# A two-layer decoder trunk: h and two of four column blocks of x turned by DMA transposes, operand tiles on multiples of 512 bytes, order from a two-way walk

## The chip, the cores and the metric

The kernel runs on one core of one Trainium2 chip. The metric is the device time of one execution in microseconds, lower is better. Five engines matter: TensorE (PE; its weight loads are listed apart as PEld), VectorE (DVE), ScalarE (ACT), GpSimd (POOL, hardly used here) and SyncE (SP), which only issues DMAs. Data come from HBM into the on-chip memory SBUF; products land in eight PSUM banks.

## What is computed

256 tokens of 2048 columns go through two layers. Layer 0 mixes tokens by causal pooling means, layer 1 by differential attention; each is followed by a SwiGLU feed-forward with 5632 inner columns. All sub-layers take a normalised input and add to x; a last norm ends it.

```python
for i in range(DEPTH):                              # 2 layers
    hn = rmsnorm(h, norm_mix[i])
    mix = pool_mixer(hn, ...) if i % 2 == 0 else diff_attention(hn, w_qkv, ..., w_o)
    h = h + mix
    h = h + swiglu(rmsnorm(h, norm_ffn[i]), w_gate[i], w_up[i], w_down[i])
return rmsnorm(h, final_norm)

def swiglu(h, wg, wu, wd):
    return (jax.nn.silu(h @ wg) * (h @ wu)) @ wd
```

Everything is float32, so the kernel splits each operand into a high and a low part in the fp32r format and multiplies high by high, high by low and low by high.

## The kernel before

**A group of products.** All large products go through `group` (L335). A group has 8 steps (6 in the short down-projection); each step takes one pair of 128-row blocks of the contraction, loads one MiB of weights into `raw` (L307, SP's queue, three buffers), splits it into `whi` (ScalarE, L313) and `wlo` (VectorE, L314), and multiplies. A plain step has 8 block products, 24 matmuls of 128 x 512. A step "by seven" uses a scheme of Strassen's kind: 7 block products, 21 matmuls, but VectorE makes sums of the weights first (`tsum`, L319 to L321) and their low parts (`tlo`, L328), ScalarE their high parts (`thi`, L327). `GATE_UP`, `SEVEN`, `SEVEN_DOWN` and the like say which steps of a group go by seven. `combined` (L395) adds the seven sums up from the PSUM banks into four tiles c (L401 to L411).

**The operand side.** The stationary operand is the activations, turned so that the contraction lies on the partitions. For x it is `xp`/`xq`, one tile for each pair of blocks, made by `transposed` (L470) from `x_tok`; for the hidden layer it is `h`, made from the tiles c after silu and product (L677, L678). Both use `pair` (L445): four TensorE transposes of 128 x 128 into a PSUM bank (L450), then either the high and the low part directly (L454, L455, or with a gain L442, L443) or, for a step by seven, an evacuation to a tile e with eight slots (L463), three VectorE sums in it (L464 to L466), a cast and a subtraction (L467, L468).

**The stages.** The pooling layer comes first. A feed-forward (L657) runs in three chunks of 4, 4 and 3 gate-and-up groups; after each chunk come the two halves (o = 0 and 1) of the down-projection over that chunk's h, 8 steps each, 6 in the last chunk. After the last chunk x is updated, one column block of 512 at a time (j = 2o + b), its squares are summed (`square_sum`, L428), and the block is turned for the next stage. Attention has four groups for q and k, two for v, and two halves of the output projection, after which x is updated and turned in the same way (L827 to L834).

**The order.** TensorE, VectorE, ScalarE and SP work in order. `in_order_of_need` (L226) fixes that order before the kernel is built: `steps_of` (L104) reads the dependences out of the program, `walk` (L162) plays it forward with assumed durations and a rank, and `due` (L213) gives each instruction a limit from TensorE's order. Two rounds are tried, TensorE and SP keep the program's rank, and the best order becomes fixed dependences. `Step` (L68) holds the assumed durations: `lasts` until the result is there, `holds` until the engine takes its next instruction.

**Tiles.** `dist_sb` and `ones` are constants of the whole kernel, `small`, `counts` and `sq` are small tiles or scratch; where they lie shifts the addresses of the operand tiles behind them.

Of the kernel before, what the change touches and what calls it, by code (L numbers as in the profile page):

```python
# [10 lines left out]
F32 = mybir.dt.float32  # L11
F32R = mybir.dt.float32r
AF = mybir.ActivationFunctionType
# [16 lines left out]
ROUNDS = 2  # L30
# [24 lines left out]
A22, A21, A11, A12, S1, S3, S2, S4 = range(8)  # L55
T1, T3, T2, T4 = range(4)

# [7 lines left out]
PER_MIB = 2500  # L65


class Step:  # L68

    def __init__(self, k, ins=None):  # L70
        self.k, self.ins, self.engine = k, ins, ins.engine if ins else POOL
        self.dma = bool(ins) and ins.opcode == "DMACopy"
# [6 lines left out]
        if self.dma:  # L79
            bytes_ = 4 * math.prod(c for _, c in ins.outs[0].ap)  # L80
            self.share = PER_MIB * bytes_ / 2 ** 20
            self.holds, self.lasts = (60 if self.engine == ACT else 330), LANDING + self.share
        elif self.engine == PE:
            n = size(ins.outs[0])
            one = 110 if ins.is_transpose else 14 + n / 2.4 if "float32r" in str(ins.ins[0].dtype) else 14 + n / 0.6
            self.holds, self.lasts = one, one + 163
        elif self.engine == DVE:
            if ins.opcode == "TensorScalarPtr":
                self.lasts = 185 + n / 0.96 if n > 8 else 159
            else:  # L90
                self.lasts = 152 + n / (1.92 if ins.opcode == "TensorCopy" else 0.96)
            self.holds = max(self.lasts - 80, 60)
        elif self.engine == ACT:
            self.lasts = 165 + n * 0.852
            if ins.opcode == "Activation" and any(hasattr(a, "ap") for a in list(ins.ins)[1:]):
                self.lasts += 100
            self.holds = max(self.lasts - 30, 60)
            if len(ins.outs) > 1:
                self.lasts, self.holds = self.lasts + 190, self.lasts + 160
        else:  # L100
            self.holds = self.lasts = 400


def steps_of(instructions):  # L104
# [3 lines left out]
    for ins in instructions:  # L108
# [15 lines left out]
        for writes, args in ((False, ins.ins), (True, ins.outs)):  # L124
            for a in args:
# [4 lines left out]
                first = ap.offset % dims[0][0]  # L130
                last = first + sum((c - 1) * s for s, c in dims[1:])
                alone = writes
                if t.space == PSUM:
                    first, last, alone = 0, 511, True
# [78 lines left out]
def due(steps, start):  # L213

    by_start = sorted(steps, key=lambda s: start[s.k])
    at, clock = {}, 0.0
    for s in by_start:
        if s.engine == PE:
            at[s.k], clock = clock, clock + s.holds
    limit = [0.0] * len(steps)  # L220
    for s in reversed(by_start):
        limit[s.k] = min([limit[k] - s.lasts - SIGNAL[steps[k].engine] for k in s.after] + [at.get(s.k, clock)])
    return limit


def in_order_of_need(tc):  # L226
# [19 lines left out]
def trunk_kernel(ctx, tc, x_n, gains, scale_in, final_in, subln, lam_in, band, counts_in, dist,  # L246
# [31 lines left out]
    dist_sb = const.tile([P, 2 * P], F32, name="dist_sb")  # L278
    ident = const.tile([P, P], F32, name="ident")
    ones = const.tile([P, P], F32, name="ones")  # L280
    nc.vector.memset(ones, 1.0)
# [146 lines left out]
    def square_sum(ss, t, j):  # L428
# [16 lines left out]
    def pair(dst, src, gains, seven):  # L445

        ps = aux((P, 2, 2, P))
        for i in range(2):
            for t in range(2):
                nc.tensor.transpose(ps[:, i, 1 - t if seven else t], src(i, t), ident)  # L450
# [11 lines left out]
        for i, at in ((0, slice(A21, A11 + 1)), (1, slice(A22, A12 + 1, A12 - A22))):  # L462
            nc.scalar.activation(e[:, at], ps[:, i], AF.Copy, scale=1.0 if gains is None else gains[i])  # L463
        nc.vector.tensor_tensor(e[:, S1:S3 + 1], e[:, A21:A11 + 1], e[:, A22:A21 + 1], ALU.subtract)  # L464
# [3 lines left out]
        nc.vector.tensor_tensor(dst[:, 1], e, f32(dst[:, 0]), ALU.subtract)  # L468

# [9 lines left out]
    with tc.tile_pool(name="start", bufs=1, reuse_waits="tile") as st:  # L479

        warm = tmp.tile([P, 8], F32, name="warm", bufs=1)
# [9 lines left out]
        counts = st.tile([P, 8], F32, name="counts")  # L491
# [26 lines left out]
        def squares(j):  # L518
            for t in range(2):
                square_sum(ss_in, t, j)  # L520
# [57 lines left out]
        def residual(g):  # L578

            cols = slice(g * 512, (g + 1) * 512)  # L580
            for t in range(2):
# [3 lines left out]
                square_sum(ss, t, g)  # L585
# [43 lines left out]
    nc.sync.dma_start(out=dist_sb, in_=dist)  # L629

    def finish(cs, ys, final_sb, ss):

        for t in range(2):
            part = tmp.tile([P, 64], F32, name="part", bufs=2)
            nc.vector.tensor_reduce(part[:, 0:1], ss[:, t, 0:2], AX.X, ALU.add)
            for b in range(2):
                for h in range(2):
# [3 lines left out]
                    sq = tmp.tile([P, 512], F32, name="sq", bufs=1)  # L641
                    at = 1 + 2 * b + h
                    nc.scalar.activation(sq[:, :S], x_at(t, first, S), AF.Square, accum_out=part[:, at:at + 1])
# [13 lines left out]
    def ffn(layer, xq, ss, next_op, next_gain):  # L657
# [3 lines left out]
        with tc.tile_pool(name=f"ffn{layer}", bufs=1, reuse_waits="tile") as hp:  # L661
            g0 = 0
            ys = []
            for c, n in enumerate(CHUNKS):
# [6 lines left out]
                for g in range(g0, g0 + n):  # L671
# [3 lines left out]
                    for t in range(2):  # L675
                        gate, up = cs[t]
                        nc.scalar.activation(gate, gate, AF.Silu, scale=r[:, t:t + 1])  # L677
                        nc.vector.scalar_tensor_tensor(up, up, r[:, t:t + 1], gate, ALU.mult, ALU.mult)  # L678
                    for i in range(2):
                        at = 2 * (g - g0) + i  # L680
                        ht = hp.tile(pair_shape(at in SEVEN_DOWN), F32R, name="h", tag=f"h{at}")
                        pair(ht, lambda k, t: cs[t][1][:, (2 * i + k) * P:(2 * i + k + 1) * P], None, at in SEVEN_DOWN)
                        hp_tiles.append(ht)
                for o in range(2):
# [13 lines left out]
                    for b, t in ((0, 0), (0, 1), (1, 0), (1, 1)):  # L698
                        j = 2 * o + b
                        nc.vector.tensor_tensor(x_at(t, j * 512), cs[t][b], x_at(t, j * 512), ALU.add)  # L700
                        if last:
                            square_sum(ss_next, t, j)
# [6 lines left out]
                        if last and t and next_op is not None:  # L709
                            transposed(next_op, j, next_gain, SEVEN_QKV)  # L710
# [8 lines left out]
    with tc.tile_pool(name="attn", bufs=1, reuse_waits="tile") as ap_, ExitStack() as heads:  # L719
        hq = heads.enter_context(tc.tile_pool(name="qk_sums", bufs=1, reuse_waits="tile"))  # L720
        at = heads.enter_context(tc.tile_pool(name="attn_tmp", bufs=2, reuse_waits="tile"))
        small = ap_.tile([P, 64], F32, name="small")
# [84 lines left out]
        for g in range(2):  # L807
            order, by_seven = LATE if g else EARLY
            cs = scaled(combined(group([(xp[p], p in by_seven, w_v[g, p]) for p in order], op_, bufs=1), op_), (r_col, r_col))
            for h in range(4 * g, 4 * g + 4):  # L810
# [6 lines left out]
                for t in range(2):  # L817
                    sq = tmp.tile([P, 512], F32, name="sq", bufs=1)[:, :E]
# [8 lines left out]
        for g in range(2):  # L827
            cs = combined(group([(oT[p], p in SEVEN_O, w_o[g, p]) for p in range(NP)], op_, bufs=1), op_)
            for b in range(2):
                j = 2 * g + b  # L830
                for t in range(2):
                    nc.vector.tensor_tensor(x_at(t, j * 512), cs[t][b], x_at(t, j * 512), ALU.add)
                    square_sum(ss_next, t, j)
                transposed(xq, j, 4, SEVEN)  # L834
# [91 lines left out]
```

## Time and profile before

| what | value |
|---|---|
| time, median of 3 runs | 1822.0 us (1821.96 to 1822.05) |
| the profiled execution | 1821.8 us |
| its span, first to last instruction | 1819.9 us |
| granted TensorE clock | 0.998 |
| TensorE busy | 1806.3 us, 8153 matmuls and transposes |
| VectorE busy | 1686.3 us |
| ScalarE busy | 1084.0 us |
| read from HBM | 352.9 MB |

The page of the profile gives busy times and their share of the span, the chain of work that ended last, and the costliest groups of instructions. A row of a group reads: line, engine, operation, what it writes and reads, shapes and count; then busy time and the mean duration of one in ns; then the idle time of the engine before them and what ended it. The durations of matmuls overlap, so the mean duration of one is more than the turn it takes in TensorE's stream. Windows give each engine's busy time in stretches of the span. A row of waits gives total, times and longest.

### The profile page before, as it was taken

The page shows a single profiled execution, that of the slowest core. Times are in us where ns is not written, and L with a number is a line of the kernel's source. Part 1 is how long each engine was busy: PE and PEld are TensorE (multiplying, and loading weights), DVE is VectorE, ACT ScalarE, POOL GpSimd, SP SyncE. Part 2 cuts the span into 40 slices and gives each one's busy share as a digit, 9 for nine tenths or more (in the row PEclk, how much of TensorE's full clock was granted, in tenths as well). Part 3 has the DMA queues.
Part 4 walks back from the last instruction along what each step waited for, and adds up shares of the span by engine and source line. Part 5 has one row for each costly group of instructions (what it writes and reads, how often), then busy time and mean ns, then how long its engine had stood idle before and what let it go on. Part 6 is the DMA issues. An engine that isn't in the chain of part 4 may idle for free.

```text
span 1819.9 us, 21122 instructions
## 1 busy us (share of the span) xinstructions
PE 1806.3 (99%) x8153; PEld 1487.6 (82%) x8153; DVE 1686.3 (93%) x1875; ACT 1084.0 (60%) x1170; POOL 0.7 (0%) x6
## 2 busy tenths in 40 slices
PE   9999999999999999999999999999999999999997
PEld 7888888888888888888888888888888888888886
DVE  7999999999999999989997889999999999999996
ACT  7656654565645566666666766665655556445663
POOL 0000000000000000000000000000000000000000
PEclk9999999999999999999999999999999999999999
DMA  6555555455555455635544445555555455555562
GB/s 267 208 185 207 187 208 208 185 208 215 201 209 187 182 208 185 225 145 185 185 176 172 184 165 194 196 208 185 214 207 203 185 208 192 210 222 192 196 220 109
DMA packets 50932, 356.37 MB, mean 196 GB/s; under 512 B 6160, under 2 KB 6288, under 8 KB 8464
## 3 DMA queue, kind: packets, MB, share of 16 engines
q1 hardware_dynamic: 49968, 353.40, 52.7%
q10 hardware_dynamic: 864, 1.63, 0.2%
q8 instruction: 64, 1.05, 0.2%
q14 instruction: 36, 0.29, 0.1%
HBM read 352.90 MB, written 2.10 MB: 195 GB/s over the span
## 4 chain that ended last, share of the span: by engine, by line
PE 98%; DVE 1%; ACT 1%; issue 0%; DVEq 0%; ACTq 0%
PE b L380 92%; PE b L450 2%; PE b L559 1%; PE b L555 1%; PE b L767 1%; PE b L798 0%; DVE wlo L314 0%; PE b L813 0%; PE b L485 0%; PE b L814 0%; PE b L530 0%; PE b L815 0%; DVE c L402 0%; DVE c L403 0%; PE b L752 0%
## 5 line engine op out<-in xcount | busy, mean ns | idle before, releaser
L380 PE MATMUL b<-whi,xp 128*128 128x512 f32 x2654 | 850.3, 392 | 0.4 <-ACT xp L467 0.3
L313 ACT CAST whi<-raw 128x1536 fp32r<-128x1536 f32 (+1 forms) x328 | 573.0, 1747 | 349.3 <-PE b L380 270.4
L314 DVE TENSOR_TENSOR wlo<-raw,whi 128x1536 fp32r<-128x1536 f32 (+1 forms) x328 | 681.3, 2077 | 69.6 <-ACT whi L313 68.4
L380 PEld LDWEIGHTS b<-whi,xp 128*128 128x128 f32 x2654 | 496.4, 188 | 104.9 <-DVE c L408 2.7
L380 PE MATMUL b<-wlo,xp 128*128 128x512 f32 x1327 | 520.1, 392 | 0.1
L327 ACT CAST thi<-tsum 128x1024 fp32r<-128x1024 f32 x254 | 266.3, 1052 | 183.9 <-DVE tsum L321 96.1
L380 PE MATMUL b<-whi,h 128*128 128x512 f32 x1108 | 349.2, 390 | 0.0
L328 DVE TENSOR_TENSOR tlo<-tsum,thi 128x1024 fp32r<-128x1024 f32 x254 | 306.5, 1216 | 2.3 <-ACT thi L327 2.0
L380 PEld LDWEIGHTS b<-wlo,xp 128*128 128x128 f32 x1327 | 249.2, 188 | 50.9 <-DVE wlo L314 0.5
L380 PE MATMUL b<-thi,xp 128*128 128x512 f32 x744 | 248.4, 390 | 0.0
L380 PEld LDWEIGHTS b<-whi,h 128*128 128x128 f32 x1108 | 207.6, 188 | 42.6 <-DVE c L408 0.2
L380 PE MATMUL b<-wlo,h 128*128 128x512 f32 x554 | 216.0, 390 | 0.1
L380 PEld LDWEIGHTS b<-thi,xp 128*128 128x128 f32 x744 | 139.4, 188 | 28.8 <-ACT thi L327 0.2
L319 DVE TENSOR_TENSOR tsum<-raw 128x1024 f32<-128x1024 f32 x127 | 154.5, 1216 | 0.6
L380 PE MATMUL b<-tlo,xp 128*128 128x512 f32 x372 | 144.9, 389 | 0.0
L380 PEld LDWEIGHTS b<-wlo,h 128*128 128x128 f32 x554 | 104.0, 188 | 21.9 <-DVE wlo L314 0.5
L320 DVE TENSOR_TENSOR tsum<-tsum,raw 128x512 f32<-128x512 f32 x127 | 86.7, 683 | 0.6
L321 DVE TENSOR_TENSOR tsum<-tsum,raw 128x512 f32<-128x512 f32 x127 | 86.7, 682 | 0.5
L380 PEld LDWEIGHTS b<-tlo,xp 128*128 128x128 f32 x372 | 69.8, 188 | 15.1
L380 PE MATMUL b<-thi,h 128*128 128x512 f32 x240 | 78.7, 389 | 0.0
L677 ACT ACTIVATE c<-c,r_tok 128x512 f32<-128x512 f32 x44 | 31.9, 724 | 63.1 <-DVE c L403 36.1
L380 PE MATMUL b<-whi,oT 128*128 128x512 f32 x216 | 69.0, 395 | 0.0
(148 smaller groups left out, 1230.7 us busy)
## 6 DMA issues: line engine op xcount, KB each, us to landing
raw<-w_gu SPq DMA_DIRECT2D x176, 1024.0 KB, 4.8
raw<-w_down SPq DMA_DIRECT2D x88, 1024.0 KB, 4.8
raw<-w_qk SPq DMA_DIRECT2D x32, 1024.0 KB, 4.8
raw<-w_v SPq DMA_DIRECT2D x16, 1024.0 KB, 4.8
raw<-w_o SPq DMA_DIRECT2D x16, 1024.0 KB, 4.7
x_tok<-x_n SPq DMA_DIRECT2D x4, 512.0 KB, 7.2
w<-pool_w SPq DMA_DIRECT2D x4, 512.0 KB, 7.7
raw<-pool_w SPq DMA_DIRECT2D x2, 1024.0 KB, 11.2
```

The lines of the kernel that those rows point to most:

```text
L313: nc.scalar.copy(hi[:, lo_block:], raw[:, lo_block:])
L314: nc.vector.tensor_tensor(lo[:, lo_block:], raw[:, lo_block:], f32(hi[:, lo_block:]), ALU.subtract)
L319: nc.vector.tensor_tensor(s, raw[:, B11:B22 + 1], raw[:, B12:B12 + 1].broadcast_to([P, 2, 512]), ALU.add)
L320: nc.vector.tensor_tensor(t[:, 0], s[:, 0], raw[:, B22], ALU.add)
L321: nc.vector.tensor_tensor(t[:, 1], t[:, 0], raw[:, B21], ALU.add)
L327: nc.scalar.copy(hi, t)
L328: nc.vector.tensor_tensor(lo, t, f32(hi), ALU.subtract)
L380: nc.tensor.matmul(ps[b], x, y[:, block], start=first, stop=(left[b] == 0))
L450: nc.tensor.transpose(ps[:, i, 1 - t if seven else t], src(i, t), ident)
L555: nc.tensor.matmul(yp[g][t], a[:, rows], w_pool[g][:, at], start=(at == 0), stop=(at == 3))
L559: nc.tensor.matmul(yp[g][t], u, v[:, at], start=(at == 0 and j == 0), stop=(at == 3 and j == 2))
L677: nc.scalar.activation(gate, gate, AF.Silu, scale=r[:, t:t + 1])
```

## The change

**Transposes by DMA.** A float32 number is moved as two 16-bit halves. `flip` copies 512 columns of a 128-token tile on ScalarE into another tile, all first halves ahead of all second halves, and SP issues a DMA that transposes the 1024 half words in blocks of 128 into a tile `turned`. `pair_of_words` puts the halves together again: ScalarE copies them from `turned` into e, with the two halves side by side, and from there the high and low parts are made as before. All of h goes this way, in both layers. Of x, the column blocks of the first half of the projection (j = 0 and 1) after the first feed-forward and after the attention go this way; j = 2 and 3 and the blocks after the pooling still use `pair`.

```diff
+    def flip(turned, t, gate, up):
+        halves_ = half_words(gate)
+        nc.scalar.copy(halves_.rearrange("p (w n) -> p w n", w=2), half_words(up).rearrange("p (n w) -> p w n", w=2))
+        nc.sync.dma_start_transpose(out=turned[:, t].rearrange("p w b n -> p (w b) n"), in_=halves_)
+
+    def pair_of_words(dst, turned, i, seven, gains=None):
+        e = tmp.tile([P, 8, P], F32, name="e", bufs=1)
+        words = half_words(e).rearrange("p b (n w) -> p b n w", w=2)
+        if seven:
+            for k, at in enumerate(PLACES):
+                nc.scalar.copy(words[:, at], turned[:, :, :, 2 * i + k].rearrange("p t w n -> p t n w"))
+                if gains is not None:
+                    nc.scalar.activation(e[:, at], e[:, at], AF.Copy, scale=gains[k])
+            seven_of(dst, e)
+            return
+        for k in range(2):
+            nc.scalar.copy(words[:, 2 * k:2 * k + 2], turned[:, :, :, 2 * i + k].rearrange("p t w n -> p t n w"))
+        both = e[:, :4].rearrange("p (k t) n -> p k (t n)", k=2)
+        if gains is not None:
+            for k in range(2):
+                split(dst[:, k], both[:, k], gains[k])
+            return
+        nc.scalar.copy(dst[:, :, 0], both)
+        nc.vector.tensor_tensor(dst[:, :, 1], both, f32(dst[:, :, 0]), ALU.subtract)
+
+    def turned_by_transfer(pool, xp, j, gain, seven, spare):
+        turned = pool.tile([P, 2, 2, 4, P], U16, name="turned")
+        for t in range(2):
+            flip(turned, t, spare[t], x_tok[:, j, t])
+        for i in range(2):
+            p = 2 * j + i
+            pair_of_words(xp[p], turned, i, p in seven, [gain_sb[:, gain, 2 * p + k:2 * p + k + 1] for k in range(2)])
...
                         nc.vector.scalar_tensor_tensor(up, up, r[:, t:t + 1], gate, ALU.mult, ALU.mult)
+                        if t == 0:
+                            turned = hp.tile([P, 2, 2, 4, P], U16, name="turned")
+                        flip(turned, t, gate, up)
                     for i in range(2):
...
-                        pair(ht, lambda k, t: cs[t][1][:, (2 * i + k) * P:(2 * i + k + 1) * P], None, at in SEVEN_DOWN)
+                        pair_of_words(ht, turned, i, at in SEVEN_DOWN)
...
-                            transposed(next_op, j, next_gain, SEVEN_QKV)
+                            if o:
+                                transposed(next_op, j, next_gain, SEVEN_QKV)
+                            else:
+                                turned_by_transfer(hp, next_op, j, next_gain, SEVEN_QKV, [cs[0][b], cs[1][b]])
...
-                transposed(xq, j, 4, SEVEN)
+                if g:
+                    transposed(xq, j, 4, SEVEN)
+                else:
+                    turned_by_transfer(op_, xq, j, 4, SEVEN, [cs[0][b], cs[1][b]])
```

The slots of e are renumbered so that the two token halves of a block stand in the order that the transfer writes:

```diff
-A22, A21, A11, A12, S1, S3, S2, S4 = range(8)
+A12, A11, A21, A22, S3, S1, S2, S4 = range(8)
```

**Places of tiles.** The scratch tile `sq` goes; the squares are written over tiles that are done with (in the last stage over the PSUM bank just read). `dist_sb` and `ones` move from the constants into the pools of the stages that use them (the DMA of dist with it), and `small` and `counts` become 128 columns wide, so that what follows them lies on a multiple of 512 bytes.

```diff
-    dist_sb = const.tile([P, 2 * P], F32, name="dist_sb")
...
-        sq = tmp.tile([P, 512], F32, name="sq", bufs=1)
         nc.scalar.activation(sq, x_at(t, j * 512), AF.Square, accum_out=ss[:, t, j:j + 1])
...
-        counts = st.tile([P, 8], F32, name="counts")
+        counts = st.tile([P, 128], F32, name="counts")[:, :8]
...
-                    nc.scalar.activation(sq[:, :S], x_at(t, first, S), AF.Square, accum_out=part[:, at:at + 1])
+                    nc.scalar.activation(cs[t][b][:, mine], x_at(t, first, S), AF.Square, accum_out=part[:, at:at + 1])
...
-        small = ap_.tile([P, 64], F32, name="small")
+        small = ap_.tile([P, 128], F32, name="small")
```

**The order.** `due` gives way to `latest`, which plays the program backward from its end with the same assumed durations, each engine taking one instruction at a time, and so gives each instruction the latest place that it can have. Up to eight rounds go backward and forward; in each, two ranks are tried, one that keeps TensorE and SP in the program's order and one that ranks them by need too. `Step` gets durations for the transposing DMA (SP is held 1290 ns; it lands 1000 ns and a share of 14 ns for each 2048 half words later) and 80 ns more for ScalarE copies with more than three dimensions.

```diff
-ROUNDS = 2
+ROUNDS = 8
...
+        if turns:
+            self.share = TURN_TILE * n * P / 2048
+            self.holds, self.lasts = 1290, 1000 + self.share
...
+    last = start
     for _ in range(ROUNDS):
-        limit = due(steps, start)
-        rank = [float(s.k) if s.engine in (PE, SP) else limit[s.k] for s in steps]
-        again, span = walk(steps, rank)
+        need = latest(steps, last)
+        both = [[float(s.k) if s.engine in (PE, SP) else need[s.k] for s in steps], need]
+        last, span = min((walk(steps, r) for r in both), key=lambda w: w[1])
         if span < end:
-            start, end = again, span
+            start, end = last, span
```

More of the change, by code (lines that the diff above doesn't have):

```diff
@@ L65 @@
 PER_MIB = 2500
+TURN_TILE = 14
 class Step:
@@ L129, in steps_of @@
                 t, dims = ap.tensor, [tuple(d) for d in ap.ap]
-                first = ap.offset % dims[0][0]
-                last = first + sum((c - 1) * s for s, c in dims[1:])
+                each = mybir.dt.size(a.dtype)
+                first = ap.offset % dims[0][0] * each
+                last = first + sum((c - 1) * s for s, c in dims[1:]) * each + each - 1
                 alone = writes
                 if t.space == PSUM:
-                    first, last, alone = 0, 511, True
+                    first, last, alone = 0, 2047, True
                 if t.name not in seen:
@@ L210, in walk, with latest @@
     return start, max(free.values())
[L213 to L223, printed above, removed]
+def latest(steps, start):
+    missing = [len(s.after) for s in steps]
+    ready, place = [0.0] * len(steps), [0.0] * len(steps)
+    engines = (PE, DVE, ACT, SP, POOL)
+    free = {e: 0.0 for e in engines}
+    able, coming = {e: [] for e in engines}, {e: [] for e in engines}
+    for s in steps:
+        if not s.after:
+            heapq.heappush(coming[s.engine], (0.0, s.k))
+    for _ in steps:
+        now, e = min((free[e] if able[e] else max(free[e], coming[e][0][0]), i)
+                     for i, e in enumerate(engines) if able[e] or coming[e])
+        e = engines[e]
+        while coming[e] and coming[e][0][0] <= now:
+            k = heapq.heappop(coming[e])[1]
+            heapq.heappush(able[e], (-start[k], -k))
+        s = steps[-heapq.heappop(able[e])[1]]
+        place[s.k] = free[e] = now + s.holds
+        for k in s.before:
+            b = steps[k]
+            if b.engine != e or b.dma:
+                after = b.lasts + SIGNAL[e] - (0 if b.dma else b.holds)
+            elif e == DVE or e == ACT and k in s.reads:
+                after = b.lasts + SETTLES[e] - b.holds
+            else:
+                after = 0.0
+            ready[k] = max(ready[k], place[s.k] + after)
+            missing[k] -= 1
+            if not missing[k]:
+                heapq.heappush(coming[b.engine], (ready[k], k))
+    end = max(place)
+    return [end - p for p in place]
 def in_order_of_need(tc):
@@ L449, in pair @@
             for t in range(2):
-                nc.tensor.transpose(ps[:, i, 1 - t if seven else t], src(i, t), ident)
+                nc.tensor.transpose(ps[:, i, t], src(i, t), ident)
         if not seven:
@@ L721, in trunk_kernel @@
         at = heads.enter_context(tc.tile_pool(name="attn_tmp", bufs=2, reuse_waits="tile"))
-        small = ap_.tile([P, 64], F32, name="small")
+        small = ap_.tile([P, 128], F32, name="small")
+        dist_sb = ap_.tile([P, 2 * P], F32, name="dist_sb")
+        nc.sync.dma_start(out=dist_sb, in_=dist)
+        ones = all_ones(ap_)
         qs_col, subln_sb, lam_sb, lp, le, neg_lam, gs = (
```

39 lines of the change are left out of this document (25 added, 14 removed).

## The prediction

> **What bounds the kernel now.** I read the page first: its busy times, its slices and its chain.
>
> ```profile
> span 1819.9 us, 21122 instructions
> PE 1806.3 (99%) x8153; PEld 1487.6 (82%) x8153; DVE 1686.3 (93%) x1875; ACT 1084.0 (60%) x1170; POOL 0.7 (0%) x6
> ...
> PEclk9999999999999999999999999999999999999999
> ...
> q1 hardware_dynamic: 49968, 353.40, 52.7%
> ...
> PE 98%; DVE 1%; ACT 1%; issue 0%; DVEq 0%; ACTq 0%
> ```
>
> TensorE is on 98% of the chain that ended last, at full granted clock, and it is idle for only 1819.9 - 1806.3 = 13.6 us. VectorE, at 93%, is close behind; ScalarE and the DMA rings have room. So what leaves TensorE's queue shortens the run, as long as VectorE can keep up with the shorter time. To see both I cut the span at the starts of the groups of products (a group is 6 or 8 loads of weights) and asked for busy time in these windows.
>
> ```profile
> core 0: us, PE busy (x) PEld busy (x) DVE busy (x) ACT busy (x) POOL busy (x), PEclk, DMA share, GB/s
> 85.70:127.40 41.70, 41.70 (x189) 34.57 (x188) 40.34 (x41) 25.01 (x22) 0.00 (x0) 1.00 0.54 197
> ...
> 211.80:254.20 42.40, 42.40 (x193) 35.09 (x192) 41.17 (x43) 23.59 (x21) 0.00 (x0) 1.00 0.54 199
> 254.20:295.70 41.50, 41.50 (x185) 34.38 (x184) 37.87 (x37) 20.90 (x16) 0.00 (x0) 1.00 0.55 203
> ...
> 421.10:463.50 42.40, 42.40 (x192) 35.11 (x191) 40.02 (x41) 24.48 (x22) 0.00 (x0) 1.00 0.54 198
> ...
> 588.30:630.00 41.70, 41.70 (x189) 34.40 (x188) 40.52 (x40) 24.91 (x22) 0.00 (x0) 1.00 0.56 202
> ...
> 672.60:704.90 32.30, 32.30 (x148) 26.73 (x147) 31.52 (x36) 19.20 (x20) 0.00 (x0) 1.00 0.55 196
> 704.90:738.00 33.10, 33.10 (x156) 27.52 (x155) 32.67 (x39) 23.48 (x31) 0.00 (x0) 1.00 0.52 191
> ...
> 1070.60:1114.50 43.90, 43.90 (x203) 36.47 (x202) 39.74 (x42) 25.93 (x33) 0.00 (x0) 1.00 0.60 222
> ...
> 1810.50:1819.90 9.40, 0.00 (x0) 0.00 (x0) 3.68 (x12) 1.95 (x6) 0.00 (x0) 0.64 0.55 212
> ```
>
> In each of these but the last, TensorE's busy time is the whole window. VectorE has 41.70 - 40.52 = 1.2 us left in a gate-and-up group with four sevens (588.30), and 0.4 us in 704.90. The last window is the tail without products; with it, 13.6 - 9.4 = 4.2 us of TensorE idle time remain in all the rest.
>
> **The change, part by part.** *TensorE's transposes.* The rows by form show them:
>
> ```profile
> L450 PE MATMUL b<-ident,c 128*128 128x128 f32 x176 | 26.3, 272 | 0.0
> ...
> L450 PE MATMUL b<-ident,x_tok 128*128 128x128 f32 x96 | 14.0, 273 | 0.0
> ```
>
> 176 is 22 groups x 2 pairs x 4 blocks: all of h. Of the 96 on x, 32 follow the pooling, 32 the first feed-forward and 32 the attention; the change takes two of four column blocks of the last two, 32 in all. Durations overlap, so I price them by windows. 211.80 and 254.20 are the two halves of the same down-projection, each 3 steps of 21 products and 5 of 24, 183 in all; only the first holds a group's 8 transposes of h: 42.40 - 41.50 = 0.90 us. 22 x 0.90 = 19.8 us. A product costs 41.50 / 183 = 0.2268 us. The window 704.90 has 2 x 21 + 4 x 24 = 138 products, 31.3 us; the 16 transposes of x make the other 1.8 us of 33.10. 1070.60 has 2 x 21 + 6 x 24 = 186, 42.2 us, and 1.7 us for its 16. Together TensorE loses 19.8 + 1.8 + 1.7 = **23.3 us** of work. The blocks that stay on TensorE are the second half of each projection, which the next stage waits for.
>
> *VectorE's work* stays: the sums of a seven and the low parts are the same instructions, reading e in place of a PSUM bank. But it gets less time. Where a group's transposes go, TensorE needs 41.70 - 0.90 = 40.80 us in 588.30 against 40.52 of VectorE. The last chunk of the first layer, 672.60 and 704.90, needs 32.30 + 33.10 - 0.9 - 1.8 = 62.7 us on TensorE and 31.52 + 32.67 = 64.2 on VectorE: there VectorE sets the end, unless work slides into a neighbour. How much idle time must remain on VectorE is seen in the waits and in time order:
>
> ```profile
> ACT whi L313 <- PE b L380: 270.4, 146, 5.5
> ...
> DVE c L402 <- PE b L380: 17.2, 17, 1.3
> ```
>
> ```profile
> 111.15 2.36 DVE L328 TENSOR_TENSOR tlo<-tsum,thi 128x1024 fp32r<-128x1024 f32 x2
> ...
> 114.06 0.39 PE L380 MATMUL b<-tlo,xp 128*128 128x512 f32 x1
> ```
>
> 17.2 / 17 = 1.0 us per group boundary is VectorE waiting for TensorE's last bank. The second tlo ends at 113.51 and its product starts at 114.06: 0.55 us of margin late in a group. If the 1.0 us stays at each boundary, the group of 588.30 overruns by 40.52 + 1.0 - 40.80 = 0.7 us, the window of 85.70 by 40.34 + 1.0 - 40.80 = 0.5, and that of 421.10 by nothing (41.0 of 41.5). At 0.4 us on average, 22 groups lose 9 us. If no such wait has to stay, the loss is the 64.2 - 62.7 = 1.5 us of the last chunk, or nothing where that slides into a neighbour. I take **4 us**, somewhat under the middle, because h's own low parts (1.28 us for two plain pairs, at 94.19 below, between two tlo) no longer have to empty a PSUM bank and can be put behind the tight products.
>
> ```profile
> 94.19 1.28 DVE L455 TENSOR_TENSOR h<-b,h 128x512 fp32r<-128x512 f32 x2
> ```
>
> *ScalarE.* Each block turned by a transfer adds two flips (128 x 1024 half words) and, for each of two pairs, two copies of 128 x 512 half words into e. No row shows half words; the nearest rows are these:
>
> ```profile
> L327 ACT CAST thi<-tsum 128x1024 fp32r<-128x1024 f32 x254 | 266.3, 1052 | 183.9 <-DVE tsum L321 96.1 <-DVE tsum L319 66.4 <-PE b L380 19.8
> ...
> L454 ACT CAST h<-b 128x512 fp32r<-128x512 f32 x28 | 16.0, 593 | 9.5 <-PE b L450 9.5
> ...
> L463 ACT ACTIVATE e<-b 128x256 f32<-128x256 f32 x32 | 10.6, 382 | 17.7 <-PE b L450 17.7
> ```
>
> By elements, 26 blocks give 52 x 1.05 + 104 x 0.59 = 116 us, less 32 x 0.38 = 12 us of evacuations: +104 us, to 1188 of some 1800, 66%. Bounds: half of it if two-byte elements go at twice the rate (+46), double if their stride costs as much again (+220, 72%). A group's ScalarE goes from 25 us by 2 x 1.05 + 4 x 0.59 = 4.5 to 29.5 of 41. I take the middle and cost it at nothing: its cover is the 270.4 us in which whi waits for buffers that TensorE frees. Without that cover each us in front of a thi would reach a tlo with 0.55 us of margin.
>
> *The transfers.* 52 transposes of 256 KB on SP's queue. No row shows one.
>
> ```profile
> raw<-w_gu SPq DMA_DIRECT2D x176, 1024.0 KB, 4.8
> ...
> scale_sb<-scale_in SPq DMA_DIRECT2D x1, 1024.0 KB, 12.1
> ...
> out_t<-y ACTq DMA_DIRECT2D x2, 256.0 KB, 2.9
> ```
>
> ```profile
> 98.83 0.33 SPq L307 DMA_DIRECT2D raw<-w_gu  x1
> ```
>
> ```profile
> SPq L307 <- DVE wlo L314: 916.1, 198, 13.3
> ```
>
> Bounds for landing: 2.9 us (the same bytes, plain) to 12.1 (four times the bytes behind others); I take 5, near a load. Bounds for SP: 0.33 us, a load's issue, to the 2.9 us of a whole landing; I take 1.3, which the diff's planner uses. Behind it stand only weight loads. SP spends 916 us waiting for VectorE to free a raw buffer, so 2 x 1.3 us per group are cover. The end of an h block then comes about 2 x 1.05 (flips) + 5 + 4 x 0.59 = 9.5 us later than before; even the last group of a chunk has its h due only after the 4 or 6 earlier pairs of the down-projection, 4 x 5 = 20 us or more. The two x blocks have a whole second half, 31 us at least, ahead of them. So this lies beside other work, at nothing; without the cover a group would pay the 9.5 us.
>
> *Places on multiples of 512 bytes, sq tiles gone, dist and ones moved.* The mean of a product on thi and xp is 390 ns and on whi and oT 395 (rows below), tiles at different places: at most 5 ns of duration hang on where a tile lies. If all of the 7491 products gained or lost that in their turn, it were 37 us; but the turn is 0.2268 us on h in 254.20 and (42.40 - 0.90) / 183 in 211.80 alike, so I take 0 and keep no more than 1 us either way.
>
> ```profile
> L380 PE MATMUL b<-thi,xp 128*128 128x512 f32 x744 | 248.4, 390 | 0.0
> ...
> L380 PE MATMUL b<-whi,oT 128*128 128x512 f32 x216 | 69.0, 395 | 0.0
> ```
>
>  In the tail of 9.40 us the squares go to PSUM in place of SBUF: 8 instructions, 0 to 0.4 us; I take 0.
>
> *The order from the two-way walk.* It moves VectorE, ScalarE and possibly TensorE in every stage. It can win at most the 4.2 us of TensorE idle time outside the tail; it can lose as much where it puts a low part late. I take 0, between -4 and +4.
>
> Sum: the profiled run took 1821.8 us, 1.9 more than its span and 0.2 under the median of 1822.0. 1821.8 - 23.3 + 4 = **1802.5 us**.
>
> **The rivals.** (1) *VectorE becomes the bound.* All 9 us of boundary waiting stay: 1821.8 - 23.3 + 9 = 1807.5. For it: 99% of VectorE in the shortened groups (40.52 of 40.80). Against: h's low parts become movable.
> (2) *The order wins as well*: VectorE loses nothing and the 4.2 us go: 1821.8 - 23.3 - 4.2 = 1794. For it: the margins are uneven, 0.55 us late in a group and none needed at its start. Against: the profile has very little idle time to win.
> (3) *Slower: ScalarE's queue waits for the turned tile.* The first copy into e of a group stands in ScalarE's order in front of whi and thi; the order is fixed from assumed landings. If the tile lands X us later than its place allows, thi and then tlo are X late, and beyond the 0.55 us of margin TensorE waits. It outweighs the saving from 0.55 + 23.3 / 22 = 1.6 us per group. At 3 us: 22 x 2.45 = 54 us lost, 1821.8 - 23.3 + 54 = 1852. For it: with load traffic at 0.55 of the rings, a transpose queues behind up to one load, 4.8 us. Against: the 270.4 / 146 = 1.9 us that an average whi waits for its buffer absorb a first delay.
> (4) *The transfers fill the rings*, so it does not do what it says. A group has 0.55 x 41 = 22.6 us of ring time in loads; two transposes exceed the rest from (41 - 22.6) / 2 = 9.2 us each. At the 12.1 us of the far row: 2 x 12.1 + 22.6 = 46.8 against 40.8, 22 x 6 = 132 us, 1930. For it, only that far row; against it, 2.9 us for equal bytes. The Trainium skill's "VectorE: DVE Perf Modes", "The three transpose paths", speaks for it: it lists 1309 ns for a 128 x 128 block by transfer against 390 ns on TensorE and advises TensorE where PSUM will do. Eight blocks at that price are an estimated 10.5 us for one flip. The trace's TensorE figure differs, 0.90 / 8 = 0.11 us for one of eight in a row; no run here shows the other. The skill's "DMA: Bandwidth & Descriptors", "Latency and other measured facts", speaks against it: 261 GB/s for transposing transfers, an estimated 1.0 us for a flip, a tenth of the first.
> (5) *No difference*: waits of about 1.1 us per group give back 23 us, 1820 to 1824; the same place as (3) at its turning point.
>
> **How the numbers follow.** Forecast 1802.5, 0.52; (1) 0.18; (2) 0.13; (3) 0.09; (4) 0.03; (5) 0.05. The forecast's own bounds are 1798.5 to 1806.5 from VectorE's 0 to 8 and the order's few us. The range takes in (1) with the order's +4, 1812, and (2) with a little more, 1793: 1793 to 1812, which leaves out (3), (4), (5), 0.17, and the edges. About 0.2% (3.6 us) is what a measurement of this kernel tells from no change. Faster: forecast, (1), (2), 0.83. Same: 0.05. Slower: 0.12.
>
> **What would show it.** Right: 176 + 32 fewer TensorE transposes; the window of a down-projection's first half as long as that of its second, 41.5 us; TensorE still on 97% or more of the chain; VectorE at 94%. If (1): waits of products on wlo and tlo grow to several us in all, and VectorE's wait for the last bank vanishes. If (3): a wait of ScalarE on the turned tile's DMA of a us or more per group, followed by waits of TensorE on tlo. If (4): DMA share near 1 and loads landing after far more than 4.8 us. My forecast is wrong if the transposes hold SP or the rings much longer than 1.3 and 5 us, if two-byte copies cost over twice 1.05 us, or if the new order moves more than the 4.2 us that I allow it.

## The result and the profile after

The changed kernel takes 1799.45 us (median of 4 runs, 1799.01 to 1800.55) against 1821.98 us (1821.96 to 1822.05): a ratio of 0.9877, interval 0.9860 to 0.9894, 22.5 us less. The forecast was 1802.5, range 1793 to 1812. The profiled execution took 1799.01 us, its span 1797.2.

The page of the changed kernel, with the lines that answer to those of before:

```profile
span 1797.2 us, 20952 instructions
...
PE 1782.2 (99%) x7945; PEld 1467.4 (82%) x7945; DVE 1680.4 (94%) x1876; ACT 1184.0 (66%) x1294; POOL 0.7 (0%) x6
...
q1 hardware_dynamic: 104880, 367.03, 58.7%
...
PE 26%; DVE 2%; DMA 1%; issue 1%; ACT 1%; DVEq 0%; SPq 0%; ACTq 0%
```

TensorE has 208 instructions less and 24.1 us less of busy time. It is idle for 1797.2 - 1782.2 = 15.0 us, of which 9.8 are the tail: 5.2 in all the rest, where it was 4.2. VectorE's busy time is nearly the same, 5.9 us less; ScalarE has 100 us more. The followed chain breaks off in this trace (its shares add up to 31%), so the 98% of before have no counterpart.

Windows of the changed kernel, cut at the starts of groups as before (span of the window, its length, then busy time of each engine, clock, DMA share, GB/s). In this order: a gate-and-up group, the two halves of a down-projection, the last half of the first layer's down-projection, the first q and k group, the second layer's first gate-and-up group, the tail.

```profile
84.80:125.70 40.90, 40.90 (x182) 33.86 (x182) 40.54 (x44) 30.96 (x30) 0.00 (x0) 1.00 0.60 216
208.00:249.50 41.50, 41.50 (x185) 34.37 (x184) 40.95 (x42) 27.64 (x25) 0.00 (x0) 1.00 0.66 225
249.50:291.00 41.50, 41.50 (x185) 34.37 (x184) 37.77 (x37) 21.00 (x16) 0.00 (x0) 1.00 0.58 209
...
693.70:725.40 31.70, 31.46 (x140) 25.75 (x138) 29.74 (x32) 30.10 (x41) 0.00 (x0) 1.00 0.77 251
725.40:770.30 44.90, 44.67 (x205) 36.71 (x205) 43.21 (x60) 30.47 (x39) 0.00 (x0) 1.00 0.59 203
...
1100.40:1144.00 43.60, 42.60 (x193) 35.02 (x192) 43.60 (x46) 29.80 (x35) 0.00 (x0) 1.00 0.58 217
1787.40:1797.20 9.80, 0.00 (x1) 0.00 (x0) 4.26 (x13) 1.95 (x6) 0.00 (x0) 0.66 0.55 209
```

And two of the kernel before that were not shown, the first q and k group and the second layer's first group:

```profile
738.00:782.40 44.40, 44.40 (x207) 36.47 (x205) 40.42 (x53) 29.80 (x36) 0.00 (x0) 1.00 0.56 203
1114.50:1157.70 43.20, 43.20 (x200) 35.94 (x199) 42.77 (x55) 31.02 (x36) 0.00 (x0) 1.00 0.49 181
```

The reader sees three things. The first half of the down-projection is as long as the second, 41.5 us, as forecast, and the groups went from 41.7 to 40.9. Two of these windows grew, 44.40 to 44.90 and 43.20 to 43.60: the groups that start right after a turning of x. And the tail grew from 9.4 to 9.8.

What the new work costs, from the groups by form, from the rows of the line that issues the transposes, and from SP's waits of the changed kernel:

```profile
L514 ACT COPY c<-c 128x1024 uint16<-128x1024 uint16 x44 | 45.4, 1043 | 8.9 <-DVE c L754 8.9
...
L523 ACT COPY e<-turned 128x512 uint16<-128x512 uint16 x36 | 23.1, 679 | 8.3 <-DMA turned<-c 8.3
```

```profile
L515 SPq DMA_TRANSPOSE turned<-c x52: 1231/1233/1320, 107.2 to 1731.0; - x52
...
DMA to landing us min/median/max: 2.7/2.7/6.7
```

```profile
SPq L515 <- ACT c L514: 159.8, 34, 10.1
SPq L515 <- ACT thi L363: 47.4, 9, 9.5
```

A flip takes 1.04 us, a copy of half words 0.68; a transposing DMA holds SP for 1.23 us and lands after 2.7. ScalarE waits for a turned tile 5 times, 8.9 us in all, 8.3 of them in the row shown. SP, however, stands in front of the transposes for 207 us in these two rows, waiting for ScalarE (159.8 us of it for the flips themselves), and the loads behind them stand with it.

### The profile page after: what moved, and what is told of

Its sections match the earlier page's. It is cut to its first block, busy times and chain, and to the rows that moved or that the text cites. A ratio compares the mean times of both kernels' runs of the same rounds, so it can differ in the third digit from the quotient of the medians.

```text
span 1797.2 us, 20952 instructions
## 1 busy us (share of the span) xinstructions
PE 1782.2 (99%) x7945; PEld 1467.4 (82%) x7945; DVE 1680.4 (94%) x1876; ACT 1184.0 (66%) x1294; POOL 0.7 (0%) x6
## 3 DMA queue, kind: packets, MB, share of 16 engines
q1 hardware_dynamic: 104880, 367.03, 58.7%
## 5 line engine op out<-in xcount | busy, mean ns | idle before, releaser
L416 PE MATMUL b<-thi,xp 128*128 128x512 f32 x744 | 254.5, 389 | 0.0
L416 PEld LDWEIGHTS b<-thi,h 128*128 128x128 f32 x240 | 45.0, 188 | 9.4
```

The lines of the kernel that those rows point to most:

```text
L416: nc.tensor.matmul(ps[b], x, y[:, block], start=first, stop=(left[b] == 0))
```

## The experiments

Twelve kernels, each against the kernel before on the same chip. "To the change" is the difference of the two distances from the kernel before, since chips differ by 0.3 us. Each kernel is ordered anew as a whole, so a difference holds both the edit and the order that came of it.

| kernel | us, median | ratio to before, interval | to the change, us |
|---|---|---|---|
| the change | 1799.45 | 0.9877, 0.9860 to 0.9894 | |
| old order | 1816.29 | 0.9969, 0.9958 to 0.9980 | +16.6 |
| new order alone | 1820.91 | 0.9993, 0.9983 to 1.0003 | +21.2 |
| TensorE and SP keep rank | 1804.01 | 0.9900, 0.9884 to 0.9917 | +4.6 |
| h only | 1801.08 | 0.9884, 0.9870 to 0.9899 | +1.4 |
| x only | 1817.22 | 0.9972, 0.9961 to 0.9983 | +17.5 |
| four blocks of x | 1823.05 | 1.0006, 0.9996 to 1.0015 | +23.6 |
| low parts twice | 1809.90 | 0.9932, 0.9918 to 0.9947 | +10.2 |
| transfers twice | 1839.58 | 1.0093, 1.0078 to 1.0108 | +40.1 |
| second transfer beside | 1810.47 | 0.9934, 0.9918 to 0.9951 | +10.9 |
| squares in SBUF | 1798.98 | 0.9873, 0.9858 to 0.9888 | -0.5 |
| fitted durations | 1800.01 | 0.9878, 0.9864 to 0.9893 | +0.3 |
| places back | 1800.17 | 0.9878, 0.9861 to 0.9894 | +0.4 |

My theory going in was that TensorE's saving is paid out but for a few us of VectorE's boundary waits, and that the order hardly matters; the rival, that the order does a large part of it.

**Old order.** The transfers and places of the change, the order made as before.

```diff
-ROUNDS = 8
+ROUNDS = 2
...
-        need = latest(steps, last)
-        both = [[float(s.k) if s.engine in (PE, SP) else need[s.k] for s in steps], need]
-        last, span = min((walk(steps, r) for r in both), key=lambda w: w[1])
+        limit = due(steps, start)
+        rank = [float(s.k) if s.engine in (PE, SP) else limit[s.k] for s in steps]
+        again, span = walk(steps, rank)
```

> The change with the order planned as before it (limits from TensorE's order, two rounds). Theory A, TensorE's removed transposes are the saving and VectorE fits into the shorter groups in either order: 1799 to 1803 us. Theory B, VectorE is the bound in the shortened groups and only the two-way walk hides it: the 4 to 9 us of the prediction appear, 1804 to 1809. Theory C, most of the saving is the order's: above 1810.

1816.29, the third case: of 22.5 us only 5.9 are left. By the planner's own reckoning its two rounds came out longer than the first walk (1822.5 us against 1811.7), so that the program's rank stands on all engines; it does so in the kernel before too (1824.6 against 1816.4). So what is compared is the order by the program's rank with that of the two-way walk. The waits of this kernel (its L415 is L438 of the change, L421 is L444, L340 is thi, L341 is tlo, L327 is wlo), then those of the change:

```profile
DVE c L415 <- PE b L393: 26.9, 23, 2.6
...
PEld b L393 <- DVE wlo L327: 10.1, 10, 2.2
PEld b L393 <- DVE c L421: 6.7, 13, 1.2
PEld b L393 <- ACT thi L340: 4.1, 4, 1.4
PEld b L393 <- DVE tlo L341: 3.8, 10, 1.0
```

```profile
DVE c L438 <- PE b L416: 10.9, 11, 3.5
...
PEld b L416 <- DVE wlo L350: 2.9, 6, 1.4
PEld b L416 <- DVE tlo L364: 1.7, 4, 1.0
PEld b L416 <- DVE c L444: 1.4, 2, 0.9
```

VectorE's wait for the last bank is 26.9 us where it was 17.2 before and is 10.9 in the change. That wait alone does not set the time: it is 16.1 us with h only and 18.0 with TensorE and SP at the program's rank, and these kernels take 1801.08 and 1804.01. What reaches TensorE shows in front of its weight loads: in the rows shown they wait 24.7 us for wlo, thi, tlo and freed banks in the old order, 6.0 in the change, 18.7 us more. VectorE's timeline at one boundary (start, length, instruction, and in brackets the idle time before it and what ended that):

```profile
621.94 1.22 DVE L341 TENSOR_TENSOR tlo<-tsum,thi 128x1024 fp32r<-128x1024 f32 x1
624.06 0.69 DVE L415 TENSOR_TENSOR c<-b,c 128x512 f32<-128x512 f32 x1 [0.90 <-PE b L393]
...
625.99 2.28 DVE L327 TENSOR_TENSOR wlo<-raw,whi 128x2048 fp32r<-128x2048 f32 x1
...
622.88 1.91 ACT L326 CAST whi<-raw 128x2048 fp32r<-128x2048 f32 x1 [1.42 <-DMA raw<-w_gu]
...
628.33 0.50 PE L393 MATMUL b<-wlo,xp 128*128 128x512 f32 x1 [0.89 <-DVE wlo L327]
...
631.20 0.50 PE L393 MATMUL b<-thi,xp 128*128 128x512 f32 x1 [0.98 <-ACT thi L340]
```

And the same boundary of the change:

```profile
615.46 1.22 DVE L364 TENSOR_TENSOR tlo<-tsum,thi 128x1024 fp32r<-128x1024 f32 x1
616.59 0.68 DVE L536 TENSOR_TENSOR h<-e,h 128x512 fp32r<-128x512 f32 x1
617.49 0.69 DVE L438 TENSOR_TENSOR c<-b,c 128x512 f32<-128x512 f32 x1 [0.22 <-PE b L416]
```

With the old order VectorE stands for 0.90 us between the last tlo and the last bank; whi waits 1.42 us for a load; wlo ends at 628.27 and TensorE waits twice, for wlo and for thi, 1.87 us in all. In the change the low part of an h pair (0.68 us) lies in that gap and 0.22 us are left. This is one boundary of many; the 16.6 us were not added up boundary by boundary.

**New order alone.** The kernel before with `latest` and eight rounds.

> The kernel before with only the two-way walk. Theory A: at most the 4.2 us of TensorE idle time outside the tail can go, 1818 to 1822 us. Theory C: 1810 or less.

1820.91, 1.3 us less than the kernel before, within what can be told from no change. So the order alone is worth little (the 1.3 us are taken below as they stand), and 16.6 us once the transfers are there.

**TensorE and SP keep the program's rank.**

```diff
-        both = [[float(s.k) if s.engine in (PE, SP) else need[s.k] for s in steps], need]
-        last, span = min((walk(steps, r) for r in both), key=lambda w: w[1])
+        last, span = walk(steps, [float(s.k) if s.engine in (PE, SP) else need[s.k] for s in steps])
```

> The change with the two-way walk, but TensorE and SP always keep the program's rank, as before; VectorE and ScalarE go by need. Theory D, the order wins by when VectorE and ScalarE do h's work: 1799 to 1802 us. Theory E, it wins by the places of the transposing DMAs and loads on SP and of TensorE's last transposes: 1808 or more, most of the way to the 1816.3 of the old order.

1804.01. Of the order's 16.6 us, 12.0 are there with VectorE and ScalarE alone by need, and 4.6 come when TensorE and SP may go by need as well.

**h only, and x only.** In the first both calls of `turned_by_transfer` are `transposed` again. In the second h goes through TensorE:

```diff
-                        if t == 0:
-                            turned = hp.tile([P, 2, 2, 4, P], U16, name="turned")
-                        flip(turned, t, gate, up)
...
-                        pair_of_words(ht, turned, i, at in SEVEN_DOWN)
+                        pair(ht, lambda k, t: cs[t][1][:, (2 * i + k) * P:(2 * i + k + 1) * P], None, at in SEVEN_DOWN)
```

> All of x turned on TensorE, h by transfers: 32 more transposes at some 0.11 us. Theory A: 3.5 us more than the change, 1803 us. If the two x blocks cost as much at the stage boundaries as they save (waits of 1.3 us at the first q and k group and 1.5 us at the first gate-and-up group of layer 1 in the trace after): 1799 to 1801.

> h turned by TensorE as before; the two column blocks of x by transfers; the new order. Of the x blocks' 3.5 us some 1.6 were left in the whole change, by the run without them. If the two parts add, this is 1.6 us under the old kernel with the new order: 1819.3 (1818.5 to 1820). If the x transfers pay in full where no h transfers stand beside them, 1817.4; if they only pay where the rest of the order has been loosened by h, 1820.5 to 1822.

1801.08 and 1817.22. Against the new order alone, h is worth 21.1 - 1.3 = 19.8 us and x 5.0 - 1.3 = 3.7: both are paid in full where the other is missing. Together they bring 22.5 - 1.3 = 21.2, so 2.3 us go when they meet: beside h, the two blocks of x add 1.4 us. The x-only run came out at the second of its three cases (1817.4).

**Four blocks of x.** `turned_by_transfer` for all four column blocks.

> All four column blocks of x turned by transfers at both places, the second halves too. TensorE loses 32 more transposes, 3.5 us. Theory A: the last blocks are on the path into the next stage, flip, landing of 2.7 us, copies and sums cost some 7 us twice: 1806 to 1815 us. Rival, the first plain steps of the next stage cover it: 1796.

1823.05, above both cases of the expectation: the whole gain is gone. Windows of this kernel, first q and k group and first group of the second layer:

```profile
732.70:781.50 48.80, 46.63 (x188) 36.06 (x188) 38.06 (x48) 35.66 (x43) 0.00 (x0) 0.94 0.55 188
1110.20:1165.40 55.20, 47.12 (x185) 36.64 (x185) 45.27 (x53) 36.94 (x44) 0.00 (x0) 0.91 0.48 163
```

And its timeline in the second, ScalarE first, then SP's queue, then TensorE:

```profile
1114.94 1.03 ACT L514 COPY c<-x_tok 128x1024 uint16<-128x1024 uint16 x1
...
1129.67 0.68 ACT L523 COPY e<-turned 128x512 uint16<-128x512 uint16 x1 [2.01 <-DVE xp L506]
...
1123.63 2.58 SPq L515 DMA_TRANSPOSE turned<-c  x2
...
1138.60 1.22 PE L416 MATMUL b<-thi,xp 128*128 128x512 f32 x2 [5.25 <-ACT thi L363]
```

The last block of x is flipped at 1114.94, 4.7 us after the group began that needs it. Its half words are copied at 1129.67, the next stage's thi stands behind it on ScalarE until 1137.51, and TensorE waits 5.25 us. Little of this is the transfer itself, which lands after 2.7 us. SP issues the block's two transposes only at 1123.63: a load ahead of them in its queue goes out at 1120.13, after a wait for wlo, and at 1123.60 ScalarE ends its last copy of the block before (1122.94, 0.66 us long) from the one tile `turned`. The copy then waits 2.01 us more for the one tile e. Whether more such tiles or another place in SP's queue would give cover was not tested.

48.80 - 44.90 + 55.20 - 43.60 = 15.5 of the 23.6 us lie in these two windows, and their granted clock of 0.94 and 0.91 is part of it. The rest is not all the blocks' own: TensorE's first 1712 matmuls and transposes are done at 388.8 us in the change and at 392.0 here, 3.2 us behind, in the first feed-forward, where both kernels do the same work in different orders.

**Low parts twice.** h's low parts are subtracted a second time, so that VectorE has 44 instructions more.

```diff
+            if twice:
+                nc.vector.tensor_tensor(dst[:, 1], e, f32(dst[:, 0]), ALU.subtract)
```

> The change with the low part of every h tile computed twice on VectorE: 28 x 0.68 + 16 x 1.22 = 38.6 us more VectorE work, 1.8 us per group. Theory A, VectorE has room because h's work can be moved (1797.2 - 1680.4 = 116.8 us of idle time in the whole span): 1800 to 1810 us. Theory B, VectorE at the bound in the groups: most of the 38.6 us, 1825 or more.

1809.90. VectorE's line on the page of this kernel:

```profile
PE 1787.5 (99%) x7945; PEld 1465.2 (81%) x7945; DVE 1712.1 (95%) x1920; ACT 1185.0 (66%) x1294; POOL 0.7 (0%) x6
```

VectorE's busy time grew by 31.7 us (the 38.6 expected is the sum of durations, and these overlap) and the run became 10.2 longer: two thirds found room. VectorE, at 94%, is not the bound of the changed kernel; of these 31.7 us it had room for about 20.

**Transfers twice, and a second transfer beside.** First every transposing DMA issued twice into the same tile; then, for h alone, the second one into `up`, which nothing reads any more.

```diff
         nc.sync.dma_start_transpose(out=turned[:, t].rearrange("p w b n -> p (w b) n"), in_=halves_)
+        if spare is not None:
+            nc.sync.dma_start_transpose(out=half_words(spare).rearrange("p (b n) -> p b n", n=P), in_=halves_)
```

> Every transposing DMA issued twice to the same place: 52 more holds of SP at 1.23 us (64 us), and the second waits for the first. Theory A, the transfers lie beside other work: 1799 to 1802 us. If SP or the landing is at the edge: each group pays part of 2 x (1.23 + 2.7) us, 1810 or more.

> The changed kernel with a second transposing DMA behind each of the 44 of h, into the tile up, which nothing reads any more. SP and the rings get the same additional work as in the run with every transfer issued twice (1839.58, +40 us), but turned is complete after its first transfer, so ScalarE's copies do not wait longer. If that run's loss comes from the turned tile landing some 4 us later in front of ScalarE's queue, this one stays near the changed kernel: 1799 to 1806. If it comes from SP standing longer and from the rings, the loss stays: 44/52 of 40 us, 1833, at least 1825. Between the two the loss is shared, and the waits of ScalarE on turned and of whi on raw say how.

1839.58 and 1810.47. Waits of the first, with one row of SP's:

```profile
ACT e L524 <- DMA turned<-c: 43.2, 14, 5.0
ACT whi L349 <- DMA raw<-w_gu: 42.0, 27, 3.9
...
SPq L516 <- DMA turned<-c: 58.5, 37, 5.3
```

Waits of the second:

```profile
ACT whi L349 <- DMA raw<-w_gu: 21.5, 16, 3.2
...
ACT e L525 <- DMA turned<-c: 20.6, 10, 5.0
```

More transfers are not free for the taking: 44 of them, with nobody waiting for their results, cost 10.9 us. They reach the rest through SP and the rings: whi's wait for loads in the row shown is 21.5 us where it is 14.4 in the change, and ScalarE's wait for turned 20.6 in place of 8.3. How much is SP's, how much the rings' and how much the new order's was not separated. The other 29 us of the first run go with what it alone has: eight more transfers, turned complete only after its second transfer (ScalarE waits 43.2 us in place of 8.3), and SP standing at the second transfer for the first (58.5 us), with the loads behind it. These weren't separated either.

**Three small ones.** Squares of the last stage in SBUF tiles of their own; the same, with the planner's durations nearer to those measured; `counts` and `small` at 8 and 64 columns again.

```diff
-                    nc.scalar.activation(cs[t][b][:, mine], x_at(t, first, S), AF.Square, accum_out=part[:, at:at + 1])
+                    nc.scalar.activation(sq[t][b][:, mine], x_at(t, first, S), AF.Square, accum_out=part[:, at:at + 1])
...
-            self.holds, self.lasts = 1290, 1000 + self.share
+            self.holds, self.lasts = 1235, 600 + self.share
...
-        counts = st.tile([P, 128], F32, name="counts")[:, :8]
+        counts = st.tile([P, 8], F32, name="counts")
```

> The squares of the last stage written to SBUF tiles in place of the PSUM bank that the next addition reads. The trace after shows additions and squares in turn there and a tail of 9.81 us in place of 9.40. If the shared bank makes the wait: the tail is 9.4 us again and the time 0.4 us less, 1799.0. If not, the tail stays at 9.8.

> The changed kernel with its last squares in SBUF, and with the durations that the order is made from nearer to those measured: a transposing DMA holds SP 1235 ns and lands 600 ns and its share later, and a ScalarE copy of more than three dimensions holds ScalarE 80 ns longer. If the order's worth hangs on durations that are right to a tenth of a us, the stalls of about 1 us each at gu1.0, gu1.3 and dn1.0.0 get shorter and the time is 1796 to 1798. If the order only has to be roughly right, 1798.5 to 1800, as with the squares in SBUF alone (1798.98). Above 1801 the planner's choice is luck within that margin.

> The changed kernel with counts and small at 8 and 64 columns again, so that the operand tiles behind them in the pooling and attention stages leave the multiples of 512 bytes. If places cost nothing, as forecast, the time is 1799 to 1800 and the windows of the attention stages are as long as in the changed kernel to 0.1 us. If they matter, the groups of pooling, qk, v and o take longer, by up to 5 ns for each of some 1600 products, 1802 to 1807, and the feed-forwards stay as they are.

1798.98, 1800.01 and 1800.17: none can be told from the change. The tail shows in the timelines, of the change and then of the squares in SBUF:

```profile
1787.44 0.42 DVE L717 TENSOR_TENSOR x_tok<-b,x_tok 128x256 f32<-128x256 f32 x1 [0.18 <-PE b L416]
1787.78 0.68 DVE L720 TENSOR_TENSOR y<-x_tok,final_sb 128x512 f32<-128x512 f32 x1
...
1788.44 0.42 DVE L717 TENSOR_TENSOR x_tok<-b,x_tok 128x256 f32<-128x256 f32 x1
```

```profile
1788.67 0.76 DVE L717 TENSOR_TENSOR x_tok<-b,x_tok 128x256 f32<-128x256 f32 x2
```

With the squares written to the bank, the second addition (1788.44) comes 1.00 us after the first, and a multiplication of 0.68 us stands between them on VectorE; in SBUF that multiplication is done ahead of them, the two follow each other, 0.76 us for both, and the tail is 9.2 us in place of 9.8. Whether the shared bank keeps the second addition back, or only the order that came of it, was not told apart.

For the places, the attention stages behind the first q and k group are one window, 770.30 to 1057.30 us in the change and 771.40 to 1058.40 with the places put back: 287.00 us in both. Only these two widths were put back; the places of `sq`, `dist_sb` and `ones` were not tried apart. No run beats the change by more than can be measured.

## Why the prediction held, and what in it was wrong

**TensorE's 23.3 us** came as priced. Its last product ends at 1787.4 in place of 1810.5, 23.1 us earlier, all waits included. Against the new order alone h is worth 19.8 us, where 22 x 0.90 = 19.8 was forecast, and x 3.7, where 1.8 + 1.7 was; the two together 21.2.

**VectorE's +4 us and the order's 0** are the step that failed. I priced them apart: VectorE's boundary waits at 4 us, up to 9, and the order at no more than the 4.2 us of idle time that TensorE had before. They are one term. Without the new order 16.6 us are given back, nearly twice the upper bound; with it, idle time outside the tail went from 4.2 to 5.2 us, 1.0 in place of 4. The 4.2 us were the wrong ceiling: an order can also keep away the waits that the change itself brings, and these were not in the trace of before. The remark beside it, that h's low parts would be movable, names the mechanism that the boundary at 616 to 618 us shows; the sum gave it no number. The price of VectorE's waits was misread as well: 17.2 us in 17 waits is 1.0 us a wait, but the row counts 17 waits in 41 groups, so 0.4 us a boundary on average. With 0.4 the overruns of 0.7 and 0.5 us that the 4 and 9 us are made of come down to 0.1 us and nothing. By the sign that the prediction itself set (wrong "if the new order moves more than the 4.2 us that I allow it") this step was wrong, and that the forecast landed 3 us off is luck: two errors of one pair cancel. The planner held the size beforehand: its walk, with the durations it assumes, puts 1811.7 us on the order by the program's rank and 1795.5 on the best round of the two-way walk, 16.2 apart.

**ScalarE** was forecast at 1188 us and has 1184.0. Half words go at the rate of float32 (1.043 against the assumed 1.05 us), the middle of the bounds; the copies into e take 0.68 in place of 0.59. The cover held.

**The transfers**: SP's hold 1.23 (1.3 taken), landing 2.7 (5 taken, 2.9 the lower bound, so a little below it). At nothing, as forecast, in the run itself. But the cover that I named for SP, 916 us of waiting for VectorE, is thinner than it looks: a second transfer behind each flip of h, with nobody waiting for its result, costs 10.9 us. What I left out is that SP stands at a transpose until ScalarE is done (207 us in the rows above), with loads behind it.

**The places** at 0 held for the two widths that were put back. **The tail**, 0 of 0 to 0.4, took 0.4, and with the squares in SBUF it is 0.6 shorter; in the time this can't be told from nothing.

**The rivals.** (1) VectorE as the bound: in the change 31.7 us more of VectorE cost only 10.2, its wait for the last bank fell by a third (17.2 to 10.9) but did not vanish. Weight loads on TensorE wait 4.6 us for wlo and tlo, where they waited 1.1 before: the sign of this rival is there, but small. In the old order it is 13.9 us. (2) The order wins as well: right in its direction, at a size that I had ruled out, but against the waits of the change, not the idle time of before. (3) ScalarE's queue waiting for the turned tile: 8.9 us in 5 waits, 0.4 us per group on average against the 1.6 at which it decides; the mechanism is there, as the transfers issued twice show, and the chain of the changed kernel passes through it once:

```profile
1730.97 6.33 DMA turned<-c
...
1743.42 1.23 DVE h L506
```

There a transfer took 6.3 us, and the down-projection's products waited 0.25 us for the h that was made from it. (4) The rings: 58.7% of 1797.2 less 52.7% of 1819.9 is 96 us for 52 transfers, 1.8 us of the rings each, a fifth of the 9.2 that would have filled them. The price in the Trainium skill's "VectorE: DVE Perf Modes", "The three transpose paths", an estimated 10.5 us for a flip of eight blocks, is not confirmed here: 2.7 us from issue to landing. The advice of the same page of the Trainium skill, under "Rules for kernel authors", to use TensorE where PSUM will do, fits the blocks that a stage waits for (four blocks of x, +23.6 us), not those with cover.

## What to carry to other kernels

When a change takes work from the bounding engine and hands it to a queue beside it, price the order together with it: the ceiling of what an order wins is not the idle time in the old trace but that plus the waits that the new work would bring. A transfer that has to queue suits what is needed a stage later and not what the next stage waits for; with these queues and single tiles the same edit won 3.7 us on two blocks of x (1.4 beside h) and lost 23.6 when carried to four. An in-order queue that waits in front of an instruction is no cover for more work in front of it: ask what stands behind, and count the wait with the issue.

## What the hardware showed that was not expected

A stall of TensorE can cost more than its length, since its granted clock can fall behind it. Windows of the kernel with four blocks of x, from the start of the second layer's first group:

```profile
1110.20:1113.30 3.10, 1.36 (x5) 0.57 (x4) 2.91 (x3) 2.70 (x6) 0.00 (x0) 1.00 0.09 19
1113.30:1115.30 2.00, 1.96 (x5) 1.57 (x6) 1.14 (x4) 1.75 (x5) 0.00 (x0) 0.56 0.46 90
1115.30:1117.30 2.00, 2.00 (x6) 1.55 (x6) 0.78 (x3) 2.00 (x2) 0.00 (x0) 0.58 0.98 406
```

After 1.7 us without products the granted clock was 0.56 to 0.58 in these two rows, some 3.5 us in all, 5 or 6 products in 2 us in place of 10 (records can be missing). Idle times of much the same length did not always do this. In the old order's kernel:

```profile
719.52 0.51 PE L393 MATMUL b<-wlo,h 128*128 128x512 f32 x1 [1.81 <-DVE wlo L327]
```

```profile
719.50:723.50 4.00, 3.98 (x18) 3.31 (x19) 4.00 (x5) 4.00 (x5) 0.00 (x0) 1.00 0.87 200
```

The clock stayed at 1.00 behind these 1.81 us, and behind 1.69 us at 1281.04 in the same run. With the transfers issued twice, four idle times of 1.94 to 2.56 us were each followed by a stretch at 0.50. The two waits of 0.89 and 0.98 us in the old order's boundary did not bring the clock down: the products after them start 0.23 us apart as always. So between about 1.7 and 1.8 us it went either way here, and the runs do not show what decides. The Trainium skill's "TensorE: Matmul & The Clock Gate", "Part 1: The HAM clock gate (the "warmup" mystery)", puts the fall after an idle window of some 3.4 us; here 1.7 us was enough once.

A transposing DMA of 256 KB lands in 2.7 us, about as soon as a plain transfer of the same bytes to HBM (2.9 us before; 2.5 and 3.8 on two queues in the change). But by an estimate from the rings' shares it takes 1.8 us of ring time, where the 353.40 MB of transfers before took 959 us, 0.7 us for 256 KB.
